# A down projection with one level of Strassen's products, its partial sums copied from bank to bank

## The chip, the core and the metric

The kernel runs on one NeuronCore of a Trainium2 chip. The metric is the device time of one execution in microseconds (us); the time of before is the median of three runs. TensorE does the matmuls into PSUM, which has eight banks here, each a tile of 128 partitions x 512 floats. VectorE and ScalarE read and write PSUM and SBUF; loads and stores are DMAs issued from the queues of SyncE (SP) and ScalarE (ACT).

## The reference

One layer of a hybrid decoder runs on 1024 prompt rows and 32 sample rows (8 sequences of 4), so on 1056 rows of 1024 channels. What is ahead of the channel mixing (two mixers, an output projection, norms) is not touched. The channel mixing is

```python
h = rms_norm(x, g_pre_ffn)
f = einsum('bsf,fd->bsd', square(relu(einsum('bsd,df->bsf', h, w_up))), w_down)
return x + rms_norm(f, g_post_ffn)
```

with w_up 1024 x 4096 and w_down 4096 x 1024. Everything is float32 in and out.

## The kernel before

**Precision.** A float32 product is made of three matmuls: each operand is split into a rounded part and the rest ("hi" and "lo", types marked fp32r), and hi·hi, hi·lo and lo·hi are summed in PSUM (`TERMS`). `split` does this: a cast on ScalarE (line 127), a subtraction on VectorE (line 128).

**Columns.** In the channel mixing rows are the moving columns. They stand in two column groups: group 0 has tiles 0 to 3 and the sample rows, 2 x 272 columns, group 1 has tiles 4 to 7, 2 x 256 columns (`SUB`). The halves of a group are the two column halves of a Strassen product.

**Up stage.** It already runs one level of Strassen (Winograd's form, seven products in place of eight). `NPAIR` = 16 pairs of row blocks, each for both groups, are 32 `Quad`s. A product is 12 matmuls (4 blocks of the inner dimension x 3 terms). Between products that accumulate on bank A, ScalarE keeps copies of A in SBUF (`snap`, line 797), and VectorE adds them later (lines 817 to 840). `first`, `second` and `third` are cut so that a Quad's first two products stand ahead of the last two of the one before. The results are squared after Relu (line 844) and stored to `f_d` in HBM, two stores for a Quad from ScalarE's queue (`store`, `flush`). `up_weights` makes the seven weight forms of a pair: four VectorE sums and seven splits.

**Down stage.** It is a plain product: `NFB` = 8 rounds of 4 row blocks of f; for each of 8 output blocks and 3 column chunks (`TB`: 400, 400 and 256 columns) `down_one` sums 12 matmuls in one of four rotating "z" banks, and VectorE adds the bank to the accumulator `acc` in SBUF (line 1077; a copy in the first round, line 1075). The next round's f blocks and weights are loaded on SyncE's queue and split meanwhile (`f_tile`, `pair`). In the last round the chunks are the outer loop, so that tiles whose columns are complete can be finished between matmuls: `Finish` transposes the accumulator on TensorE, squares on ScalarE (line 1105), multiplies with the gain on VectorE (line 1106), scales and adds x (line 1119) and stores. Seven of the nine tiles are finished inside; tiles 6 and 7 have their first half inside and their second half after the last matmul.

**Order.** Matmuls, transposes and DMAs keep the order in which the program issues them on their queue (`keep_in_program_order`). The order of VectorE's and ScalarE's instructions is fixed when the kernel is built; each engine runs its own in that order and waits at an instruction whose operands are not ready. A tile pool with `bufs=n` gives a buffer out again when its last reader is done.

Of the kernel before, what the change touches and what calls it, by code (L numbers as in the profile page):

```python
# [39 lines left out]
TB = [(0, 3 * P + NSH), (3 * P + NSH, 3 * P + NSH), (6 * P + NS, 2 * P)]  # L40
TBT = [(0, 1, 2), (NCH, 3, 4, 5), (6, 7)]
# [4 lines left out]
def hymba_step(ctx: ExitStack, tc: tile.TileContext, a: dict):  # L46
# [24 lines left out]
    hpool1 = ctx.enter_context(tc.tile_pool(name="hpool1", bufs=1, side="right"))  # L71
# [3 lines left out]
    stage = ctx.enter_context(tc.tile_pool(name="stage", bufs=3))  # L75
    psum = ctx.enter_context(tc.tile_pool(name="psum", bufs=4, space=PSUM))
# [18 lines left out]
    f_d = [dpool.tile([P, T], F32, name="f_d%d" % ft) for ft in range(NFT)]  # L95
# [673 lines left out]

    class Quad:  # L770
# [72 lines left out]
        def emit(self, i, f):  # L843
            vec.scalar_tensor_tensor(f, f, 0.0, f, ALU.max, ALU.mult)  # L844
            c0 = GBASE[self.g]
            store(f_d[2 * self.p + i][:, c0:c0 + 2 * self.n].rearrange("p (s c) -> p s c", s=2), f)
# [176 lines left out]
    def f_tile(ft):  # L1023
        f = f_pools[0 if ft % 9 < 7 else 1].tile([P, 2, T], F32R, name="f")
        for g in range(2):
            c = slice(GBASE[g], GBASE[g] + GW[g])
            raw = raw_load(f_d[ft][:, c], [P, GW[g]])
            split(f[:, 0, c], f[:, 1, c], raw)
        return f
# [4 lines left out]
    q0.sums()  # L1034
    ws_up = {0: wup0, 1: up_weights(wraw1)}
    prev = q0
    for i, (p, g) in enumerate(seq):
# [3 lines left out]
        flush()  # L1041
        if prev.g == 1:
# [7 lines left out]
        if i == len(seq) - 2:  # L1050
            psg0.close()
            phg0.close()
            f_pools.append(pq.enter_context(tc.tile_pool(name="fp", bufs=7, side="right", reuse_waits="tile")))
            fs0 = [f_tile(ft) for ft in range(FB)]
            ws0 = pair(a["w_down"][0, 0])
# [3 lines left out]
    flush()  # L1059
    pph.close()  # L1060
    pcm.close()

    with ExitStack() as pf:
        pf.enter_context(pq)
        f_pools.append(pf.enter_context(tc.tile_pool(name="fp2", bufs=2, reuse_waits="tile")))
        accp = pf.enter_context(tc.tile_pool(name="accp", bufs=1, reuse_waits="tile"))
        rp = pf.enter_context(tc.tile_pool(name="rp", bufs=2, reuse_waits="tile"))
        acc = accp.tile([P, KT, T], F32, name="acc")

        def down_one(b, fs, w, d, c0, n):  # L1070
            ps = zbank()
            run(gemm3([ps[:, :n]], [hl(w, k) for k in range(FB)], [[hl(f, slice(c0, c0 + n))] for f in fs]))
            o = acc[:, d, c0:c0 + n]
            if b == 0:
                vec.tensor_copy(o, ps[:, :n])
            else:
                vec.tensor_tensor(o, ps[:, :n], o, ALU.add)  # L1077

        class Finish:
            def __init__(self, t):  # L1080
                self.t, self.r = t, rows(t)
                self.tp = []
# [3 lines left out]
                self.ssq2 = small.tile([P, 2], F32, name="ssqo")  # L1086
                if t == NCH:
                    self.av = rp.tile([P, KT, NS], F32, name="av", bufs=1)
                    vec.tensor_copy(self.av.rearrange("p k (s c) -> p k s c", s=2),
                                    acc[:, :, 0:GW[0]].rearrange("p k (s c) -> p k s c", s=2)[:, :, :, 2 * P:])  # L1090

            def cols(self, d):
                if self.t == NCH:
                    return self.av[:, d]
                g, c = gcol(self.t)
                return acc[:, d, GBASE[g] + c.start:GBASE[g] + c.stop]

            def half(self, h):
                r = self.r
                hs = slice(h * 512, (h + 1) * 512)  # L1100
                tp = tbank()
                for k in range(4):
                    transpose(tp[:r, k * P:(k + 1) * P], self.cols(4 * h + k), P)
                junk = rp.tile([P, 512], BF16, name="rl")
                act.activation(junk[:r], tp[:r], AF.Square, scale=D ** -0.5, accum_out=self.ssq2[:r, h:h + 1])
                vec.tensor_tensor(self.y[:r, hs], tp[:r], g_fin[:r, hs], ALU.mult)  # L1106
# [16 lines left out]
        def round_weights(b, dps):  # L1123
            return [w for dp in dps for w in pair(a["w_down"][b, dp])]

        fs, ws = fs0, ws0 + round_weights(0, range(1, KT // 2))
        for b in range(NFB):
            last = b + 1 == NFB
            if not last:
                nxt = ([f_tile((b + 1) * FB + i) for i in range(FB)], round_weights(b + 1, range(KT // 2)))  # L1130
                for d in range(KT):
                    for c0, n in TB:
                        down_one(b, fs, ws[d], d, c0, n)
                fs, ws = nxt
            else:
                g_fin = unit().bitcast(F32).rearrange("p a b -> p (a b)")
# [128 lines left out]
```

## Time and profile before

| | |
|---|---|
| median of 3 runs | 1096.48 us (1095.11 to 1099.24) |
| the profiled execution's own time | 1095.61 us |
| its span, first to last instruction | 1093.9 us |
| mean granted TensorE clock | 0.997 of full speed |
| TensorE / VectorE / ScalarE busy | 1065.0 / 680.1 / 428.2 us |

A share of busy time is a mean over stages. TensorE's matmuls are pipelined, so the duration of one (323 ns, say) is longer than the distance from one to the next; rates are read from how often a fixed piece of work recurs. Idle time of an engine that isn't the bound costs nothing.

### The profile page before, as it was taken

The page shows a single profiled execution, that of the slowest core. Times are in us where ns is not written, and L with a number is a line of the kernel's source. Part 1 is how long each engine was busy: PE and PEld are TensorE (multiplying, and loading weights), DVE is VectorE, ACT ScalarE, POOL GpSimd, SP SyncE. Part 2 cuts the span into 40 slices and gives each one's busy share as a digit, 9 for nine tenths or more (in the row PEclk, how much of TensorE's full clock was granted, in tenths as well). Part 3 has the DMA queues.
Part 4 walks back from the last instruction along what each step waited for, and adds up shares of the span by engine and source line. Part 5 has one row for each costly group of instructions (what it writes and reads, how often), then busy time and mean ns, then how long its engine had stood idle before and what let it go on. Part 6 is the DMA issues. An engine that isn't in the chain of part 4 may idle for free.

```text
span 1093.9 us, 17859 instructions
## 1 busy us (share of the span) xinstructions
PE 1065.0 (97%) x7053; PEld 996.2 (91%) x7053; DVE 680.1 (62%) x1338; ACT 428.2 (39%) x936; POOL 50.7 (5%) x77
## 2 busy tenths in 40 slices
PE   7999999999999999999999999999999999999996
PEld 5788877887787899999999999999999999999996
DVE  5777886886667897566565563575463544635257
ACT  6588874656344553323323322433030211302012
POOL 1100002120100100000000000000000000000001
PEclk9999999999999999999999999999999999999998
DMA  8432301134533334333333332554150432406034
GB/s 273 149 108 78 97 25 51 47 107 148 182 120 122 111 111 126 117 96 102 118 90 107 118 94 76 186 168 145 50 157 17 142 89 68 147 10 222 1 95 165
DMA packets 52227, 121.35 MB, mean 111 GB/s; under 512 B 6944, under 2 KB 16640, under 8 KB 52128
## 3 DMA queue, kind: packets, MB, share of 16 engines
q1 hardware_dynamic: 33312, 89.44, 27.1%
q10 hardware_dynamic: 18832, 30.78, 7.5%
q8 instruction: 55, 0.90, 0.3%
q14 instruction: 28, 0.23, 0.1%
HBM read 89.43 MB, written 31.82 MB: 111 GB/s over the span
## 4 chain that ended last, share of the span: by engine, by line
PE 85%; DVE 7%; ACT 4%; issue 2%; DMA 1%; POOL 1%; SPq 0%; DVEq 0%; ACTq 0%; POOLq 0%
PE z L64 72%; PE t L64 10%; PE t L67 3%; ACT sc L527 1%; ACT w L130 1%; DVE hn L973 1%; DVE w L128 1%; DVE w L1106 1%; DVE xr L967 1%; DVE pT L128 0%; DVE w L1119 0%; POOL ro L143 0%; DMA raw<-in_w_down_dram 0%; DVE w L131 0%; DMA raw<-in_w_qkv_dram 0%
## 5 line engine op out<-in xcount | busy, mean ns | idle before, releaser
L64 PE MATMUL z<-f,w 128*128 128x400 f32 (+1 forms) x2304 | 372.1, 323 | 0.0
L64 PEld LDWEIGHTS z<-f,w 128*128 128x128 f32 x2304 | 369.6, 188 | 0.7 <-DVE acc L1077 0.4
L64 PE MATMUL z<-w,hT_hi 128*128 128x512 f32 (+1 forms) x768 | 210.2, 380 | 0.4 <-DVE raw L191 0.4
L1077 DVE TENSOR_TENSOR acc<-z,acc 128x400 f32<-128x400 f32 (+1 forms) x168 | 87.0, 522 | 139.9 <-PE z L64 139.8
L64 PEld LDWEIGHTS z<-w,hT_hi 128*128 128x128 f32 x768 | 133.7, 188 | 25.2 <-DVE raw L191 0.8
L64 PE MATMUL z<-hT_hi,w 128*128 128x272 f32 (+1 forms) x768 | 146.8, 286 | 1.4 <-ACT s L797 1.4
L64 PE MATMUL z<-w,hT_lo 128*128 128x512 f32 (+1 forms) x384 | 124.5, 378 | 0.0
L64 PEld LDWEIGHTS z<-hT_hi,w 128*128 128x128 f32 x768 | 122.0, 189 | 1.7 <-ACT s L797 1.6
L127 ACT CAST f<-raw 128x544 fp32r<-128x544 f32 x64 | 38.6, 633 | 190.3 <-PE z L64 143.8
L64 PE MATMUL z<-hT_lo,w 128*128 128x272 f32 (+1 forms) x384 | 109.4, 285 | 0.0
L64 PE MATMUL z<-sg,w 128*128 128x272 f32 (+1 forms) x768 | 105.1, 286 | 0.6 <-ACT s L797 0.6
L64 PEld LDWEIGHTS z<-sg,w 128*128 128x128 f32 x768 | 98.7, 190 | 1.3 <-ACT s L797 1.1
L797 ACT COPY s<-z 128x256 f32<-128x256 f32 (+1 forms) x93 | 35.3, 379 | 129.0 <-PE z L64 126.1
L64 PEld LDWEIGHTS z<-w,hT_lo 128*128 128x128 f32 x384 | 67.6, 188 | 14.0
L64 PEld LDWEIGHTS z<-hT_lo,w 128*128 128x128 f32 x384 | 72.8, 190 | 0.0
L128 DVE TENSOR_TENSOR w<-w 128x512 fp32r<-128x512 f32 x64 | 43.7, 691 | 30.7 <-ACT w L127 29.5
L128 DVE TENSOR_TENSOR f<-raw,f 128x544 fp32r<-128x544 f32 x64 | 43.9, 705 | 20.0 <-ACT f L127 19.9
L128 DVE TENSOR_TENSOR w<-raw,w 128x512 fp32r<-128x512 f32 x68 | 44.0, 686 | 18.8 <-ACT w L127 18.7
L127 ACT CAST w<-raw 128x512 fp32r<-128x512 f32 x68 | 38.8, 618 | 39.6 <-DMA raw<-in_w_down_dram 34.6
L64 PE MATMUL t<-sg,w 128*128 128x272 f32 (+1 forms) x384 | 52.8, 287 | 0.6 <-DVE fo L818 0.6
L64 PE MATMUL t<-hT_hi,w 128*128 128x272 f32 (+1 forms) x256 | 52.2, 285 | 0.0
L844 DVE SCALAR_TENSOR_TENSOR fo<-fo 128x544 f32<-128x544 f32 (+1 forms) x64 | 45.3, 708 | 10.8 <-ACT fo L837 8.4
(214 smaller groups left out, 1274.8 us busy)
## 6 DMA issues: line engine op xcount, KB each, us to landing
raw<-in_w_down_dram SPq DMA_DIRECT2D x32, 512.0 KB, 4.2
rw<-in_w_up_dram SPq DMA_DIRECT2D x28, 512.0 KB, 3.9
f_d<-fo ACTq DMA_DIRECT2D x32, 272.0 KB, 3.1
raw<-f_d SPq DMA_DIRECT2D x32, 272.0 KB, 2.8
f_d<-fo ACTq DMA_DIRECT2D x32, 256.0 KB, 2.9
raw<-f_d SPq DMA_DIRECT2D x32, 256.0 KB, 2.7
xT<-in_xT_prompt_dram SPq DMA_DIRECT2D x8, 512.0 KB, 5.6
raw<-in_x_prompt_dram SPq DMA_DIRECT2D x8, 512.0 KB, 4.7
```

The lines of the kernel that those rows point to most:

```text
L64: tc.keep_in_program_order(pe.matmul(out, lhsT, rhs, start=start, stop=stop, skip_group_check=resumed))
L67: tc.keep_in_program_order(pe.transpose(out, in_, ident[:n, :n]))
L127: pin(act.copy(hi, src))
L128: pin(vec.tensor_tensor(lo, src, hi.bitcast(F32), ALU.subtract))
L130: act.activation(hi, src, AF.Copy, scale=scale)
L527: act.activation(scs[kv][:, j, 0:nk], scs[kv][:, j, 0:nk], AF.Exp, scale=-1.0, bias=nm[:, h:h + 1], accum_out=lsum[:, h:h + 1])
L797: act.copy(s, self.A)
L844: vec.scalar_tensor_tensor(f, f, 0.0, f, ALU.max, ALU.mult)
L967: vec.tensor_tensor(xr[:r], hn[:r], xr[:r], ALU.add)
L973: vec.scalar_tensor_tensor(hn[:r], xr[:r], r2[:r], g_ffn[:r], ALU.mult, ALU.mult)
L1077: vec.tensor_tensor(o, ps[:, :n], o, ALU.add)
L1106: vec.tensor_tensor(self.y[:r, hs], tp[:r], g_fin[:r, hs], ALU.mult)
```

## The change

The down projection becomes one level of Strassen too. A round (`NR` = 8) takes two pairs of row blocks, which are the two inner blocks. For each of two output halves `c` and the two column groups, `step` runs the seven products, each of 12 matmuls: two output blocks `j` x two inner blocks `k` x three terms. A step uses all eight banks as four pairs A, D, C, B. Product 1 goes to A and is copied by ScalarE to C (`fork`); product 6 is added on A and A is copied to B; products 2, 7, 3 and 4 are added on C, A, B and A, product 5 has D to itself. Matmuls thus accumulate on what ScalarE has written. `gather` adds D, C, E (A after product 7), B and A to five accumulators in SBUF on VectorE; in round 0 ScalarE copies them instead. `combine` adds D to B and E at the end. `renew` is a matmul of 512 columns that writes a whole bank: four at the start, two in the last step, after transposes have used the banks. The pairs of banks change roles from step to step.

The seven forms of f are made in the up stage: `third` gets four more VectorE sums and `stores` writes seven pieces for a Quad, from SyncE's queue. `f_load` reads back seven forms for each pair and group in three pieces and splits them; three sets of f tiles rotate. `down_weights` makes seven weight forms for each round and half with the up stage's `up_weights`; the weight array is laid out for it on the host. Five tiles are finished inside the last two steps, tiles 4 to 7 after the last matmul.

```diff
-f_d = [dpool.tile([P, T], F32, name="f_d%d" % ft) for ft in range(NFT)]
+f_d = [[dpool.tile([P, 7, n], F32, ...) for g, n in enumerate(SUB)] for p in range(NPAIR)]
...
         def third(self):
             self.product(4, self.A, False, True)
             act.activation(self.fa[:, 1], self.A, AF.Relu)
-            self.emit(0, self.fa)
+            square(self.fa)
             self.product(3, self.B, False, True)
             vec.tensor_tensor(self.fb[:, 0], self.B, self.s2, ALU.add)
-            self.emit(1, self.fb)
+            square(self.fb)
+            n = self.n
+            s = stage.tile([P, D], F32, name="raw")[:, 0:3 * n].rearrange("p (i c) -> p i c", i=3)
+            f11, f21, f12, f22 = self.fa[:, 0], self.fa[:, 1], self.fb[:, 0], self.fb[:, 1]
+            vec.tensor_tensor(s[:, 0], f21, f22, ALU.add)
+            vec.tensor_tensor(s[:, 1], s[:, 0], f11, ALU.subtract)
+            vec.tensor_tensor(s[:, 2], f11, f21, ALU.subtract)
+            vec.tensor_tensor(f21, f12, s[:, 1], ALU.subtract)
+            self.forms = [(1, f11), (5, s[:, 0]), (6, s[:, 1]), (2, f12), (7, s[:, 2]), (3, f21), (4, f22)]
+
+        def stores(self):
+            d = f_d[self.p][self.g]
+            for i, f in self.forms:
+                load(d[:, POS[i]], f)
...
+    def f_load(fs, pool_=None):
+        tiles, r, g = fs
+        n = SUB[g]
+        for a0, a1 in ((0, 2), (2, 4), (4, 7)):
+            for f, p in zip(tiles, (2 * r, 2 * r + 1)):
+                raw = (pool_ or stage).tile([P, D], F32, name="raw")[:, 0:(a1 - a0) * n]...
+                load(raw, f_d[p][g][:, a0:a1])
+                split(f[:, a0:a1, 0], f[:, a0:a1, 1], raw)
+        return tiles
+
+    def down_weights(r, c, tiles):
+        for i, t in enumerate(tiles):
+            load(t, a["w_down"][2 * r + c, i])
+        return up_weights(tiles)
...
         if i == len(seq) - 2:
...
-            fs0 = [f_tile(ft) for ft in range(FB)]
-            ws0 = pair(a["w_down"][0, 0])
+            fs0 = f_load(f_tiles(0, 0, 0))
+        if i == len(seq) - 1:
+            wdn0 = down_weights(0, 0, stage_raws())
...
+        def step(r, c, g, fs, ws, inserts=(), renewed=()):
+            n = SUB[g]
+            A, D_, C, B = [[b[:, 0:n] for b in banks[2 * i:2 * i + 2]] for i in range(4)]
+
+            def product(i, bs, start):
+                w = ws[i].rearrange("p s (k c) -> p s k c", k=4)
+                for j in range(2):
+                    for k in range(2):
+                        for m, (x, y) in enumerate(TERMS):
+                            mm(bs[j], w[:, x, 2 * k + j], fs[k][:, POS[i], y], ...)
+
+            def gather(key, bs):
+                for j in range(2):
+                    o = gacc(key, g)[:, 2 * c + j]
+                    if r == 0:
+                        act.copy(o, bs[j])
+                    else:
+                        vec.tensor_tensor(o, bs[j], o, ALU.add)
+
+            def fork(dst):
+                for j in range(2):
+                    act.copy(dst[j], A[j])
...
+            product(1, A, True)
+            fork(C)
+            product(5, D_, True)
+            gather("D", D_)
+            insert(0, 6)
+            product(6, A, False)
+            if 1 in renewed:
+                renew(banks[6:8], ws[1])
+            fork(B)
+            product(2, C, False)
+            gather("C", C)
+            insert(1, 2)
+            product(7, A, False)
+            gather("E", A)
+            product(3, B, False)
+            gather("B", B)
+            insert(2, 4)
+            product(4, A, False)
+            gather("A", A)
+            banks[:] = banks[2:4] + banks[0:2] + banks[6:8] + banks[4:6]
...
+        renew(banks[4:8], wdn0[1])
+        f_cur = [fs0, f_load(f_tiles(0, 0, 1), frp)]
+        for r in range(NR):
...
+            if r + 1 < NR:
+                w_cur.append(down_weights(r, 1, stage_raws()))
+                prefetch(0)
+                step(r, 0, 0, f_cur[0], w_cur[0])
+                step(r, 0, 1, f_cur[1], w_cur[0])
+                w_nxt.append(down_weights(r + 1, 0, stage_raws()))
+                step(r, 1, 0, f_cur[0], w_cur[1])
+                prefetch(1)
+                step(r, 1, 1, f_cur[1], w_cur[1])
             else:
...
+                step(r, 1, 0, f_cur[0], w_cur[1])
+                combine(0)
+                step(r, 0, 1, f_cur[1], w_cur[0], [(1, finish(0)), (2, finish(1))])
+                step(r, 1, 1, f_cur[1], w_cur[1],
+                     [(0, finish(2)), (1, finish(3)), (2, finish(NCH))], (1,))
+        combine(1)
+        for pair_ in ((4, 5), (6, 7)):
+            fts = [Finish(t) for t in pair_]
+            for h in range(2):
                 for ft in fts:
+                    ft.half(h, banks[0])
+                    banks[:] = banks[1:] + banks[:1]
```

## Rows read from the trace of the kernel before

**Rows 1.** The page's first part: busy us, share of span, instructions.

```profile
PE 1065.0 (97%) x7053; PEld 996.2 (91%) x7053; DVE 680.1 (62%) x1338; ACT 428.2 (39%) x936; POOL 50.7 (5%) x77
```

**Rows 2.** Busy time by stretch: length, engines' busy us, granted clock, DMA share, GB/s.

```profile
478.56:499.19 20.63, 20.63 (x170) 20.63 (x169) 12.50 (x22) 6.99 (x15) 0.00 (x0) 1.00 0.35 105
752.00:1040.00 288.00, 287.97 (x1786) 287.34 (x1786) 134.10 (x243) 53.71 (x92) 0.00 (x0) 1.00 0.31 96
```

**Rows 3.** Timeline of ScalarE, up stage: start us, us, engine, line, operation.

```profile
457.93 0.39 ACT L837 ACTIVATE fo<-z 128x256 f32<-128x256 f32 x1 [0.65 <-PE z L64]
...
478.56 0.39 ACT L837 ACTIVATE fo<-z 128x256 f32<-128x256 f32 x1 [0.65 <-PE z L64]
```

**Rows 4.** Timeline of VectorE, down stage, every third add.

```profile
962.33 0.57 DVE L1077 TENSOR_TENSOR acc<-z,acc 128x400 f32<-128x400 f32 x1 [1.77 <-PE z L64]
...
968.12 0.57 DVE L1077 TENSOR_TENSOR acc<-z,acc 128x400 f32<-128x400 f32 x1 [1.76 <-PE z L64]
```

**Rows 5.** Groups by shape, down stage: count, busy us, mean ns, idle before.

```profile
L1077 DVE TENSOR_TENSOR acc<-z,acc 128x400 f32<-128x400 f32 x86 | 49.2, 573 | 81.6 <-PE z L64 81.6
L128 DVE TENSOR_TENSOR w<-raw,w 128x512 fp32r<-128x512 f32 x48 | 30.9, 686 | 13.5 <-ACT w L127 13.4
...
L1077 DVE TENSOR_TENSOR acc<-z,acc 128x256 f32<-128x256 f32 x42 | 17.7, 421 | 16.7 <-PE z L64 16.7
L128 DVE TENSOR_TENSOR f<-raw,f 128x544 fp32r<-128x544 f32 x24 | 17.3, 722 | 6.3 <-ACT f L127 6.3
```

**Rows 6.** Groups by shape, up stage.

```profile
L797 ACT COPY s<-z 128x272 f32<-128x272 f32 x29 | 11.2, 387 | 39.4 <-PE z L64 39.4
...
L825 DVE TENSOR_TENSOR fo<-z,s 128x272 f32<-128x272 f32 x9 | 3.9, 434 | 0.0
```

**Rows 7.** Timeline where the up stage ends and the down stage begins.

```profile
697.23 0.69 DVE L844 SCALAR_TENSOR_TENSOR fo<-fo 128x512 f32<-128x512 f32 x1
...
701.02 1.14 ACT L127 CAST w<-raw 128x512 fp32r<-128x512 f32 x2 [1.84 <-DMA raw<-in_w_down_dram]
...
702.48 0.39 PE L64 MATMUL z<-hT_hi,w 128*128 128x256 f32 x1 [1.43 <-ACT s L797]
...
705.45 22.79 PE L64 MATMUL z<-f,w 128*128 128x400 f32 x140
```

**Rows 8.** Timeline of VectorE, down stage, while weights are prepared.

```profile
945.02 0.57 DVE L1077 TENSOR_TENSOR acc<-z,acc 128x400 f32<-128x400 f32 x1 [0.91 <-PE z L64]
945.81 1.29 DVE L128 TENSOR_TENSOR w<-raw,w 128x512 fp32r<-128x512 f32 x2 [0.21 <-ACT w L127]
949.07 1.29 DVE L128 TENSOR_TENSOR w<-raw,w 128x512 fp32r<-128x512 f32 x2 [1.97 <-ACT w L127]
950.28 0.57 DVE L1077 TENSOR_TENSOR acc<-z,acc 128x400 f32<-128x400 f32 x1
```

**Rows 9.** Waits, 705 to 1083 us: total us, times, longest us.

```profile
DVE f L128 <- ACT f L127: 16.2, 26, 1.5
DVE w L128 <- ACT w L127: 16.1, 14, 3.1
```

**Rows 10.** The page's DMA issues: count, KB each, us from issue to landing.

```profile
raw<-in_w_down_dram SPq DMA_DIRECT2D x32, 512.0 KB, 4.2
...
raw<-f_d SPq DMA_DIRECT2D x32, 272.0 KB, 2.8
```

**Rows 11.** The end: two lines by shape (1040 to 1094 us), two of the timeline.

```profile
L1106 DVE TENSOR_TENSOR w<-t,w 128x512 f32<-128x512 f32 x16 | 10.4, 682 | 2.4 <-ACT rl L1105 2.4
...
L67 PE MATMUL t<-ident,acc 128*128 128x128 f32 x64 | 8.6, 274 | 1.6 <-DVE acc L1077 1.6
...
1079.75 3.09 PE L64 MATMUL z<-f,w 128*128 128x256 f32 x24
...
1088.20 2.74 DVE L1119 SCALAR_TENSOR_TENSOR w<-w,ro,raw 128x512 f32<-128x512 f32 x4 [0.66 <-POOL ro L143]
```

More of the change, by code (lines that the diff above doesn't have):

```diff
@@ L94, in hymba_step @@
     x2_d = dpool.tile([T, D], F32, name="x2_d")
-    f_d = [dpool.tile([P, T], F32, name="f_d%d" % ft) for ft in range(NFT)]
+    f_d = [[dpool.tile([P, 7, n], F32, name="f_d%d_%d" % (p, g)) for g, n in enumerate(SUB)] for p in range(NPAIR)]
     kv_d = dpool.tile([NS, 2 * P], F32, name="kv_d")
@@ L768, in hymba_step, with square @@
     sg = [None, None]
+    def square(f):
+        vec.scalar_tensor_tensor(f, f, 0.0, f, ALU.max, ALU.mult)
     class Quad:
@@ L1021, in hymba_step, with f_tiles, stage_raws @@
     f_pools = []
[L1023 to L1029, printed above, removed]
+    def f_tiles(s, r, g):
+        n = SUB[g]
+        return [f_pools[s].tile([P, 7, 2, SUB[0]], F32R, name="f")[:, :, :, 0:n] for _ in range(2)], r, g
+    def f_load(fs, pool_=None):
[3 more added lines that the diff above has]
+            for f, p in zip(tiles, (2 * r, 2 * r + 1)):
+                raw = (pool_ or stage).tile([P, D], F32, name="raw")[:, 0:(a1 - a0) * n].rearrange("p (i c) -> p i c", c=n)
+                load(raw, f_d[p][g][:, a0:a1])
[5 more added lines that the diff above has]
+        return up_weights(tiles)
+    def stage_raws():
+        return [stage.tile([P, D], F32, name="raw") for _ in range(2)]
+    q0.sums()
+    ws_up = {0: wup0, 1: up_weights(wraw1)}
     last = NPAIR - 2
@@ L1041, in hymba_step @@
         flush()
+        prev.stores()
         if prev.g == 1:
@@ L1058, in hymba_step @@
     q.third()
-    flush()
+    q.stores()
     pph.close()
     pcm.close()
+    phg1.close()
     with ExitStack() as pf:
@@ L1066, in hymba_step @@
         accp = pf.enter_context(tc.tile_pool(name="accp", bufs=1, reuse_waits="tile"))
+        frp = pf.enter_context(tc.tile_pool(name="frp", bufs=2, reuse_waits="tile"))
         rp = pf.enter_context(tc.tile_pool(name="rp", bufs=2, reuse_waits="tile"))
[L1068 to L1077, printed above, removed]
+        accs = {k: accp.tile([P, 4, SUB[0] + SUB[1]], F32, name="acc%s" % k) for k in "ACBED"}
@@ L1121, in end, with finish, go, combine @@
                 flush()
[L1123 to L1134, printed above, removed]
-            else:
-                g_fin = unit().bitcast(F32).rearrange("p a b -> p (a b)")
-                load(g_fin, a["g_post_ffn"].to_broadcast([P, D]))
+        def finish(t):
+            def go(bs):
+                ft = Finish(t)
+                for h in range(2):
+                    ft.half(h, bs[h])
+                ft.scale()
+                ft.end()
+            return go
+        def combine(g):
+            for k in "BE":
+                vec.tensor_tensor(gacc(k, g), gacc(k, g), gacc("D", g), ALU.add)
+        renew(banks[4:8], wdn0[1])
+        f_cur = [fs0, f_load(f_tiles(0, 0, 1), frp)]
+        w_cur = [wdn0]
+        sets = 2
+        for r in range(NR):
+            f_nxt, w_nxt = [], []
+            def prefetch(g):
+                nonlocal sets
+                if r + 1 < NR:
+                    f_nxt.append(f_load(f_tiles(0 if sets % 3 < 2 else 1, r + 1, g), frp))
+                    sets += 1
+            if r + 1 < NR:
+                w_cur.append(down_weights(r, 1, stage_raws()))
[6 more added lines that the diff above has]
+                step(r, 1, 1, f_cur[1], w_cur[1])
+            else:
+                w_cur.append(down_weights(r, 1, stage_raws()))
+                step(r, 0, 0, f_cur[0], w_cur[0])
                 for name in ("k", "v"):
@@ L1211, in _layout @@
     w_up = w_up.reshape(NPAIR, 2, 2, P, 512)
-    w_up = np.stack([np.concatenate([w_up[:, 0, 1], w_up[:, 0, 0]], axis=-1),
-                     np.concatenate([w_up[:, 1, 0], w_up[:, 1, 1]], axis=-1)], axis=1)
+    w_down = inp["w_down"][0].reshape(NR, 2, 2, P, 2, 2, 2, P).transpose(0, 5, 4, 2, 3, 1, 6, 7)
+    w_down = w_down.reshape(2 * NR, 2, 2, P, 512)
+    w_up, w_down = [np.stack([
+        np.concatenate([w[:, 0, 1], w[:, 0, 0]], axis=-1),
+        np.concatenate([w[:, 1, 0], w[:, 1, 1]], axis=-1)], axis=1) for w in (w_up, w_down)]
     return {
@@ L1242, in _layout @@
         "w_up": c(w_up),
[L1243 to L1244 removed]
+        "w_down": c(w_down),
     }
```

88 lines of the change are left out of this document (40 added, 48 removed).

## The prediction

> **What bounds the kernel now.** I read the totals of the page first, then the busy time by stretch, then the groups of the down stage kept apart by shape, then the timeline where the two stages meet and at the end. The reader should see first that TensorE is the bound: busy 97% of the span, VectorE 62% [rows 1]. In the stretches inside the up and the down stage TensorE is busy for the whole stretch at full granted clock [rows 2], so there is no wait to remove there: only fewer or shorter matmuls help, and any new wait costs its full length. VectorE is busy 134.1 of 288.0 us in the down stage, under half.
>
> **The gain.** The up stage already runs the scheme that the down stage gets: seven products of 12 matmuls, 272 columns for column group 0 and 256 for group 1. Two such sets (168 matmuls) take 478.56 − 457.93 = 20.63 us, by the start of the same Relu one set pair apart [rows 3], with TensorE never idle [rows 2]. After the change the down stage is 8 rounds x 2 output halves x 2 column groups = 32 steps of 84 matmuls of just these widths: 16 x 20.63 = 330.1 us. Today it is 64 row-block and output-block pairs of 36 matmuls, each 968.12 − 962.33 = 5.79 us [rows 4], 370.4 us. To this come transposes inside the stage. 64 take 8.6 us [rows 11], 0.134 each; 40 remain inside (five tiles finished inside instead of seven, all halves): 5.4 us. Six renewing matmuls of 512 columns are not in the trace; a 400-column one takes about 0.18 us (5.79 us is 24 of these and 12 of 256 columns at 3.09 / 24 = 0.13 or less [rows 11]), so they are about 0.23 each, 1.4 together. New: 336.9 us. Old, from the first down matmul at 705.45 [rows 7] to the end of the last at 1079.75 + 3.09 = 1082.84 [rows 11]: 377.4 us. TensorE's own work shrinks by **40.5 us**. The columns fall by one eighth but the number of matmuls rises from 2304 to 2688, which is why 12.5% of columns become 10.9% of time.
>
> **What the other engines get.** VectorE per round (four steps, 41.26 us of TensorE):
> - 40 adds from PSUM to the accumulators, 20 of 272 columns (434 ns [rows 6]) and 20 of 256 (421 ns [rows 5]): 17.1 us. Today a round has 24, 16 of 400 columns at 573 ns and 8 of 256: 12.5 us.
> - two weight sets, each 7 subtractions and 4 sums of 512 columns at 686 ns [rows 5]: 15.1 us. Today 8 subtractions, 5.5 us.
> - activation splits: seven forms in place of four blocks. Per column group four subtractions of two forms (about 544 columns, 722 ns [rows 5]) and two of three forms; 272 more columns add about 0.28 us (573 − 421 = 152 ns for 144 columns), so 1.0 us: 4.9 us, twice: 9.7 us.
>
> Together 41.9 us, 102% of TensorE's 41.26. Back to back an instruction starts before the last one's row has ended: from the two subtractions at 949.07 to the add at 950.28 it is 1.21 us [rows 8], 0.605 each against rows of 0.686. With 0.08 us less for each of 74 instructions the round is 36.0 us. So VectorE goes from under half to between **87% and 102%** of TensorE's time in the six steady rounds.
>
> [...]
>
> **Where VectorE reaches TensorE.** Every bank is in use. The adds of the product before last and of the last must be done before the next product on the same bank. Since banks come in pairs filled one after the other, an add has half a product and one product of room: 0.74 + 1.47 = 2.2 us (one product is 20.63 / 14). Today four rotating banks give over 5 us. The trace shows what matters: at 947.10 VectorE had nothing running and waited 1.97 us for a weight cast; the add due one 2.2 us block after the one at 945.02 began only at 950.28, 3 us late [rows 8]. TensorE did not notice; with 2.2 us of room it would. Over the old stage VectorE waits 16.2 + 16.1 us behind ScalarE's casts [rows 9], 3.5 us in each 41 us, and most such casts were themselves waiting for a load. I also expect the load to be uneven: the first step of a round has the second weight set (nine of its eleven instructions, about 6 us), the rest of the last activation split (2 us), the start of the next (1.3 us) and its own adds; those due by the end of the sixth product add 3.3 us. That is 12.6 us by single rows, 10.8 back to back, wanted in some 9.9 us.
> Price per steady round: at best nothing (36.0 us fit, and prefetched forms can wait for a lighter step); at worst 41.9 + 3.5 − 41.3 = 4.1 us, and 1.6 us more if the overflow of the first step isn't won back, 5.7. I take 2.0, below the middle since the old stage's delayed adds still came between the prefetch's pairs and back to back [rows 8]: 6 x 2.0 = **12 us** (0 to 34).
>
> **ScalarE.** Per step four copies of a bank into another; no row copies PSUM to PSUM. The nearest, PSUM to SBUF, takes 387 ns for 272 columns [rows 6]; I take that, with nothing and twice that as ends. A pair, 0.78 us, must fit the same 2.2 us. ScalarE's round is 16 x 0.39 + 14 x 0.62 + 12 casts at about 0.7 = 23 us of 41: hidden, except when a cast waiting for a load sits ahead of the copy, as at 702.48, where TensorE waited 1.43 us for a copy behind casts that waited 1.84 us for w_down [rows 7]. That is in the ends above. [...]
>
> **Up stage.** Each set adds four VectorE sums of 272 columns, at most 0.43 us each: 12.5 + 3.4 = 15.9 us of 20.63 [rows 2]. No product waits for them within 10 us; seven stores per set move from ScalarE's queue to SyncE's, ahead of the next weights' load, which has a set's time to spare. 0 (0 to 3).
>
> **Handover and round 0.** The weights of the first step now need both raw tiles and eleven VectorE instructions before form 5 exists; their loads stand on SyncE behind the stores of the last set but one. That set's square ends at 697.92 [rows 7]; four sums, 1.7 us, to 699.6; the load 4.2 us [rows 10] to 703.9; cast and subtraction to 705.2, in time for product 1; form 5 comes four VectorE instructions, one cast and one subtraction later, at 709.3 against 706.9: 2.4 us late at best. The six activation loads ahead of them share three buffers, two turns of 2.8 [rows 10] + 1.4 us, which makes this later; take 5. Round 0's second activation set is loaded through buffers that lie where the up stage's tiles lay, in three turns of about 4.2 us: take 2 more. **7 us** (2 to 14).
>
> **Last round and tail.** The last round also has heavy first steps and one renewal that waits for VectorE's last reader: **3 us** (0 to 6). Today 11.1 us pass from the last down matmul to the end of the span, with two tiles to finish. Then four remain: two adds 0.85, two sums of 1024 columns 2.5, eight products with the gain at 0.68 [rows 11] 5.5, eight halves of the last step at 0.69 (four in 2.74 [rows 11]) 5.5, small ones 0.6: 15.0 us on VectorE, 3 us for the last store as now (1093.9 − 1090.94), 1.6 for work left over: 19.6, **+8.5** (+5 to +12).
>
> **Sum**, against the profiled execution's own 1095.61 us (0.9 under the median shown): 1095.6 − 40.5 + 12 + 7 + 3 + 8.5 = 1085.6, so **1086 us**. All lower ends give 1062, all upper ones 1124.
>
> **Rivals.**
> 1. *It flows like the up stage*: no steady loss, short handover, about 1070 us (1085.6 − 12 − 4). For: the up stage's TensorE never idles. Against: VectorE has 61% there, 87% or more here. 16%.
> 2. *Gain given back*: VectorE's delays cost about 3.7 us in each steady round, 1095 us: no change. For: 3.5 us of waiting behind casts per round today. 25%.
> 3. *VectorE becomes the bound: slower.* Place: the adds that free the accumulating banks in each round's first step. Price 5.7 us a round: 1085.6 + 6 x 3.7 = 1108. It decides from 4.7 us a round on (1102 us). For: 102% by single rows. Against: back-to-back starts and the lighter steps. 25%.
> 4. *The products run slower than in the up stage* (narrow matmuls bound by weight loads, say): excluded nearly by [rows 3], 1%.
>
> **How the numbers follow.** My forecast, 1077 to 1091, gets 33%; with rival 1 faster by over 0.5% (about what a measurement of this kernel can tell from no change, some 5.5 us) has 49%, no change 25%, slower 26% with rival 4. The range leaves out the far ends: 1067 to 1109.
>
> **What would show it.** Right: 32 steps near 10.3 us of matmul work, VectorE above 85% there, TensorE's few idle spells released by VectorE's adds and falling in each round's first step; an idle spell of some us where f first meets w; a tail near 20 us. Wrong: TensorE idle behind ScalarE's bank copies or behind loads in every step, bank copies well over 0.39 us, the granted clock falling between steps, or waits in the up stage for the stores.

## The result, and the profile after

The kernel after takes **1167.22 us** (median of 4 runs, 1166.81 to 1167.91) against 1096.18 us for the kernel before beside it: ratio 1.0644, 95% interval 1.0622 to 1.0666. Forecast were 1086 us and a range of 1067 to 1109: wrong in sign, and outside the range. The profiled execution took 1167.12 us, its span is 1165.4 us, its mean granted clock 0.967 (0.997 before).

I cut the span at three points: the first down matmul (705.45 us before [rows 7], 752.06 after), the end of the last one (1082.84 and 1145.07) and the end of the span (1093.9 and 1165.4).

| stage | before | after | difference | forecast |
|---|---|---|---|---|
| all up to the first down matmul | 705.45 | 752.06 | +46.6 | +5 |
| down stage | 377.4 | 393.0 | +15.6 | -23.5 |
| tail | 11.1 | 20.3 | +9.2 | +8.5 |

(The forecast column sorts the prediction's terms: 5 of the handover's 7 us stand ahead of the first down matmul; -40.5 + 12 + 2 + 3 = -23.5 in the down stage.) Two stages are wrong by some 40 us each.

The page's totals of after, to be held against [rows 1]:

```profile
PE 1060.0 (91%) x7443; PEld 982.7 (84%) x7443; DVE 833.1 (71%) x1707; ACT 531.7 (46%) x1184; POOL 50.8 (4%) x77
```

and its busy time by stretch, one in the up stage, one of four down rounds, to be held against [rows 2]:

```profile
380.00:745.00 365.00, 334.25 (x2610) 331.09 (x2608) 239.60 (x466) 109.48 (x243) 0.86 (x1) 0.96 0.39 127
...
866.00:1058.00 192.00, 173.77 (x1352) 171.60 (x1352) 150.83 (x299) 85.28 (x169) 0.00 (x0) 0.96 0.38 125
```

TensorE, which was idle for 1.2 of the 320 us from 380 to 700 us before and for none inside the down stage [rows 2], now stands for 31 of 365 and 18 of 192 us, and the granted clock is 0.96: part of its busy time is at a lower clock too. The waits of after say for whom it stands (total us, times, longest us; the first two lines are from the up stage, the others from the down stage):

```profile
PE z L64 <- ACT s L801: 18.3, 8, 3.7
PE z L64 <- ACT w L128: 11.3, 2, 5.8
...
PE z L64 <- DVE accE L1126: 21.6, 6, 4.0
PE z L64 <- DVE accA L1126: 7.9, 5, 6.6
PE z L64 <- ACT t L1130: 2.5, 4, 1.1
```

**Up stage.** TensorE waits for ScalarE's copies of bank A, 18.3 us where before it waited 0.6 us for one such copy (380 to 700 us). The 11.3 us of the second line are two waits for the weights themselves (5.80 us up to 419.14 and 5.54 us up to 710.83), each behind a cast that waited over 4 us for its load. The timeline around one of the waits for a copy in after:

```profile
634.36 0.87 SPq L51 DMA_DIRECT2D rw<-in_w_up_dram  x2
...
638.56 1.14 ACT L128 CAST w<-rw 128x512 fp32r<-128x512 f32 x2 [3.85 <-DMA rw<-in_w_up_dram]
...
642.35 2.18 ACT L128 CAST w<-w 128x512 fp32r<-128x512 f32 x4 [2.35 <-DVE w L901]
...
644.95 0.36 ACT L801 COPY s<-z 128x256 f32<-128x256 f32 x1
645.36 2.93 PE L64 MATMUL z<-sg,w 128*128 128x256 f32 x12 [3.71 <-ACT s L801]
```

The load of a pair's weights is issued at 634.36 and ScalarE waits 3.85 us for it. Behind that stand the sums of the weight forms on VectorE and four casts that wait for them; the 0.36 us copy comes last in ScalarE's fixed order, and TensorE has stood 3.71 us by then. Then 12 matmuls take 2.93 us, at a granted clock of 0.50; 12 of the same width take 1.60 at 1.00 (from 638.62). Why the load is issued so late is on SyncE's queue (a line is a run of DMAs; the last ones of a run of 14 stores):

```profile
491.33 0.80 SPq L51 DMA_DIRECT2D f_d<-raw  x2
492.18 0.44 SPq L51 DMA_DIRECT2D f_d<-fo  x1
...
497.63 0.88 SPq L51 DMA_DIRECT2D f_d<-fo  x2
498.60 0.88 SPq L51 DMA_DIRECT2D rw<-in_w_up_dram  x2
```

Around these rows a store occupies the queue for 0.33 to 0.45 us once its data are there, and it waits there for VectorE's squares and sums until they are. From 380 to 715 us the queue waits 84.6 us in 26 times for the first of the four new sums alone, which itself needs the set's last squares. In before the same queue held only loads (380 to 720 us), issued ahead; its ten waits from 437 to 521 us are all for VectorE's last reads of their buffers:

```profile
437.39 82.86 SPq L51 DMA_DIRECT2D rw<-in_w_up_dram  x9
```

**Down stage.** One long wait a round, in rounds 2 to 6 at the last product of the round's first step, which adds on the banks that accE is read from. (Round 1's comes in the step after: 6.60 us up to 821.67, for accA, behind preparation that fills VectorE from 811.96 to 820.49.) The timeline of one in after:

```profile
902.74 1.14 ACT L128 CAST w<-raw 128x512 fp32r<-128x512 f32 x2 [2.17 <-DMA raw<-in_w_down_dram]
903.39 1.29 DVE L129 TENSOR_TENSOR w<-raw,w 128x512 fp32r<-128x512 f32 x2 [2.01 <-ACT w L128]
...
907.64 2.49 DVE L129 TENSOR_TENSOR w<-w 128x512 fp32r<-128x512 f32 x4
...
910.65 1.35 DVE L129 TENSOR_TENSOR f<-raw,f 128x544 fp32r<-128x544 f32 x2
911.92 0.78 DVE L1126 TENSOR_TENSOR accD<-z,accD 128x272 f32<-128x272 f32 x2
912.62 0.78 DVE L1126 TENSOR_TENSOR accC<-t,accC 128x272 f32<-128x272 f32 x2
913.32 0.78 DVE L1126 TENSOR_TENSOR accE<-z,accE 128x272 f32<-128x272 f32 x2
913.80 6.38 PE L64 MATMUL z<-f,w 128*128 128x272 f32 x38 [4.04 <-DVE accE L1126]
```

From 903.39 to 911.92 VectorE does nothing but weights and activation splits. Six adds stand behind them, and then run back to back. TensorE stands 4.04 us for the fifth. The same wait ends at 865.72, 913.80, 961.18, 1007.90 and 1056.55: a round is (1056.55 - 865.72) / 4 = 47.7 us, 6.4 over its 41.26 us of matmuls. Busy time in steps of 2 us shows the rest of that price (the third figure from the end is the granted clock):

```profile
910.00:912.00 2.00, 0.00 (x0) 0.00 (x0) 2.00 (x5) 0.60 (x1) 0.00 (x0) 1.00 0.00 0
912.00:914.00 2.00, 0.20 (x1) 0.20 (x2) 2.00 (x7) 0.00 (x0) 0.00 (x0) 0.95 0.75 205
914.00:916.00 2.00, 2.00 (x9) 2.00 (x10) 1.64 (x5) 0.76 (x2) 0.00 (x0) 0.50 0.37 148
916.00:918.00 2.00, 2.00 (x14) 2.00 (x14) 1.44 (x3) 0.92 (x2) 0.00 (x0) 0.70 0.68 184
918.00:920.00 2.00, 2.00 (x19) 2.00 (x18) 0.59 (x3) 1.36 (x3) 0.00 (x0) 1.00 1.03 401
```

After 4 us of standing still TensorE goes on at a granted clock of 0.50: 23 matmuls begin in the 4 us from 914, where 38 would at the rate after 918. That is some 1.6 us on top of a wait of 4, an estimate from these counts.

**Tail.** 20.3 us, as priced: four tiles are left, eight halves, and VectorE, busy 16.0 us of it, does them one after the other.

### The profile page after: what moved, and what is told of

It reads as the page before. It is cut to its first block, busy times and chain, and to the rows that moved or that the text cites. A ratio compares the mean times of both kernels' runs of the same rounds, so it can differ in the third digit from the quotient of the medians.

```text
span 1165.4 us, 19447 instructions
## 1 busy us (share of the span) xinstructions
PE 1060.0 (91%) x7443; PEld 982.7 (84%) x7443; DVE 833.1 (71%) x1707; ACT 531.7 (46%) x1184; POOL 50.8 (4%) x77
## 3 DMA queue, kind: packets, MB, share of 16 engines
q1 hardware_dynamic: 70176, 132.72, 34.8%
## 5 line engine op out<-in xcount | busy, mean ns | idle before, releaser
L64 PE MATMUL z<-f,w 128*128 128x272 f32 (+1 forms) x1920 | 263.5, 295 | 39.4 <-DVE accE L1126 21.6
L64 PEld LDWEIGHTS z<-f,w 128*128 128x128 f32 x1920 | 252.2, 198 | 45.0 <-DVE accE L1126 23.0
L64 PE MATMUL z<-hT_hi,w 128*128 128x272 f32 (+1 forms) x768 | 153.5, 294 | 11.9 <-ACT w L128 11.3
L128 ACT CAST f<-raw 128x544 fp32r<-128x544 f32 (+3 forms) x96 | 67.3, 707 | 96.5 <-DMA raw<-f_d 65.7
L129 DVE TENSOR_TENSOR f<-raw,f 128x544 fp32r<-128x544 f32 (+3 forms) x96 | 75.2, 795 | 42.0 <-ACT f L128 41.6
L64 PE MATMUL t<-f,w 128*128 128x272 f32 (+1 forms) x768 | 104.1, 285 | 0.0
L64 PEld LDWEIGHTS t<-f,w 128*128 128x128 f32 x768 | 97.9, 189 | 0.0
L128 ACT CAST w<-w 128x512 fp32r<-128x512 f32 x128 | 71.0, 617 | 51.2 <-DVE w L901 46.2
L129 DVE TENSOR_TENSOR w<-w 128x512 fp32r<-128x512 f32 x128 | 80.3, 683 | 0.2 <-ACT w L128 0.2
L1130 ACT COPY t<-z 128x256 f32<-128x256 f32 (+1 forms) x128 | 46.6, 366 | 68.1 <-PE z L64 64.8
```

What stands on the lines that cost most here:

```text
L64: tc.keep_in_program_order(pe.matmul(out, lhsT, rhs, start=start, stop=stop, skip_group_check=resumed))
L128: pin(act.copy(hi, src))
L129: pin(vec.tensor_tensor(lo, src, hi.bitcast(F32), ALU.subtract))
L1130: act.copy(dst[j], A[j])
```

## The experiments

The kernel before ran beside each group of runs at 1096.47 us (experiments 1, 2, 4 and 5), 1096.72 (3, 6, 7 and 8), 1096.65 (9, 10 and 11) and 1096.68 (12).

**1. The loads ahead of the stores** (`e1_loads_first`): the weights' loads of the up stage are issued before the seven stores.

```diff
+        raws = up_raws(prev.p + 2) if prev.g == 1 and prev.p + 2 < NPAIR else None
         prev.stores()
         if prev.g == 1:
             del ws_up[prev.p]
-            if prev.p + 2 < NPAIR:
-                ws_up[prev.p + 2] = up_weights(up_raws(prev.p + 2))
+            if raws:
+                ws_up[prev.p + 2] = up_weights(raws)
```

> The changed kernel with one edit in the up stage: the two loads of the next weights are put on SyncE's queue ahead of the seven stores of the set that has just ended, not behind them. Queue theory: the up stage's loss of some 45 us comes from these loads, which stand behind fourteen stores that wait for VectorE; ScalarE's casts then wait for them with the bank copies behind. It expects 1125 to 1145 us and TensorE's waits for the bank copies (18 us in the changed kernel) mostly gone. VectorE theory (the four added sums and their buffers hold the up stage up): 1160 us or more, waits as they were.

1132.49 us, ratio 1.0329 (1.0313 to 1.0344): 34.7 us less than after, by one move on a queue. The first down matmul comes at 716.18 and not 752.06; the down stage stays as it was (393.8 us to 1109.93). TensorE's waits up to 715 us in this run:

```profile
PE z L64 <- ACT s L801: 3.4, 4, 1.0
PE t L64 <- ACT w L128: 1.9, 1, 1.9
```

The 18.3 us behind copies are 3.4, and the two long waits for weights are gone. ScalarE itself still waits 41.5 us for these loads (43.4 in after): what went is not its waiting, but that the copies stand behind it. Since the engines' orders are fixed when the kernel is built, moving the loads also moved the casts among the copies; the run doesn't separate these two.

**2. The four sums alone** (`e2_before_sums`): the kernel before with the four VectorE sums for each set, results unused.

```diff
         def third(self):
...
+            vec.tensor_tensor(s[:, 0], f21, f22, ALU.add)
+            vec.tensor_tensor(s[:, 1], s[:, 0], f11, ALU.subtract)
+            vec.tensor_tensor(s[:, 2], f11, f21, ALU.subtract)
+            vec.tensor_tensor(s[:, 0], f12, s[:, 1], ALU.subtract)
```

> The kernel before with the four added VectorE sums of each set alone, into a staging buffer that nobody reads; stores, loads and the whole down stage as before. It computes nothing new. Queue theory: no change, 1094 to 1099 us, since VectorE stays under 80% in the up stage. VectorE theory: 1115 us or more, with TensorE waiting in the up stage.

1097.57 us, ratio 1.0014 (1.0004 to 1.0023). By themselves the sums cost some 1 us: hidden, nearly as forecast.

**3. The queue alone** (`e8_before_sync_stores`): the kernel before with its two stores for each set on SyncE's queue.

```diff
-            store(f_d[2 * self.p + i][:, c0:c0 + 2 * self.n].rearrange(...), f)
+            load(f_d[2 * self.p + i][:, c0:c0 + 2 * self.n].rearrange(...), f)
```

> The kernel before with one edit: the two stores of each set are issued from SyncE's queue, in line with the loads, not from ScalarE's. Nothing else of the change is in it. Queue theory: the next weights' loads now stand behind stores that wait for VectorE, and the up stage loses some time, 1102 to 1130 us (fewer stores than in the change, and ready earlier). If the queue matters only together with the four sums: 1094 to 1100 us.

1107.89 us, ratio 1.0096 (1.0067 to 1.0125), all of it ahead of the down stage: the first down matmul is at 718.11, the down stage takes 377.4 us as in before. Its queue:

```profile
480.32 8.02 SPq L51 DMA_DIRECT2D f_d<-fo  x4
488.43 0.91 SPq L51 DMA_DIRECT2D rw<-in_w_up_dram  x2
```

The loads stand 8 us behind four stores (14 stores in after). Two stores a set on the wrong queue cost 11 us without any of the new work. ScalarE's order is fixed anew when this kernel is built, so this run doesn't separate the late loads from that order either.

**4. The preparation one step later** (`e3_prefetch_later`): each group of loads and splits is written after the step that it stood ahead of.

```diff
-                w_cur.append(down_weights(r, 1, stage_raws()))
-                prefetch(0)
                 step(r, 0, 0, f_cur[0], w_cur[0])
+                w_cur.append(down_weights(r, 1, stage_raws()))
                 step(r, 0, 1, f_cur[1], w_cur[0])
-                w_nxt.append(down_weights(r + 1, 0, stage_raws()))
+                prefetch(0)
                 step(r, 1, 0, f_cur[0], w_cur[1])
...
```

> The changed kernel with the preparation of weights and activation forms written one step later in each round of the down stage, so that the accumulator adds of the step in front come first on VectorE; the same instructions in all. Order theory (the adds wait behind a burst of preparation in each round's first step, 4 us, and the granted clock falls afterwards): 1115 to 1140 us, no wait of TensorE for the add of E above 2 us. Load theory (VectorE has simply too much work in a round): 1155 to 1170 us, the wait turns up in another step.

1159.82 us, ratio 1.0581 (1.0564 to 1.0598), only 7.4 us less. The long waits for accE are gone, but TensorE now waits 13.9 us in 12 waits for ScalarE's copies from bank to bank and 9.9 us in 11 for accA. The burst was moved, not spread. By its time and by the wait that turns up elsewhere this is the load theory's side (1155 to 1170), and so is the next run (1120 or more); experiment 6 decides between them.

**5. Both** (`e4_both`): experiments 1 and 4 together.

> Both edits of the two other kernels of the changed down stage: loads ahead of the stores in the up stage, preparation one step later in the down stage. If queue and order theory hold and their gains add: 1070 to 1100 us, at or under the kernel before. If VectorE's amount of work is what counts: 1120 us or more.

1121.02 us, ratio 1.0228 (1.0211 to 1.0245): the two add (34.7 + 7.4 = 42.1, measured 46.2). The waits of this run, at most 1.82 us from 760 to 1050 us, leave the clock there at 1.00. Two lines of this run, a step of 2 us by busy time and the wait that falls into it:

```profile
944.00:946.00 2.00, 0.27 (x3) 0.06 (x1) 2.00 (x4) 2.00 (x5) 0.00 (x0) 1.00 0.00 0
946.00:948.00 2.00, 1.91 (x16) 1.91 (x17) 2.00 (x6) 0.04 (x1) 0.00 (x0) 1.00 0.03 8
```

TensorE stood 1.82 us until 946.09 and went on at 1.00.

**6. The adds first** (`e5_adds_first`): experiment 1, and the copies from bank to bank and the adds into the accumulators get priority over the preparation in the order of their engines.

```diff
-                    if r == 0:
-                        act.copy(o, bs[j])
-                    else:
-                        vec.tensor_tensor(o, bs[j], o, ALU.add)
+                    with tc.high_priority():
+                        if r == 0:
+                            act.copy(o, bs[j])
+                        else:
+                            vec.tensor_tensor(o, bs[j], o, ALU.add)
...
-                    act.copy(dst[j], A[j])
+                    with tc.high_priority():
+                        act.copy(dst[j], A[j])
```

> The changed kernel with the loads ahead of the stores in the up stage, and in the down stage ScalarE's bank copies and the accumulator adds given a higher priority in the fixed order than the preparation of weights and forms; preparation written where the change has it. Base of comparison: the kernel with the loads ahead alone, 1132.5 us. Order theory (the adds and copies stand behind preparation that they need not wait for): 1085 to 1105 us, no wait of TensorE for the add of E above 1.5 us, granted clock at full speed in the six middle rounds. Load theory (VectorE has too much work): 1120 us or more.

1103.55 us, ratio 1.0055 (1.0037 to 1.0073), 28.9 us less than experiment 1; the down stage falls from 393.8 to 365.3 us (716.02 to 1081.36). VectorE's timeline in the heavy part of a round, in this run:

```profile
910.80 0.68 DVE L904 TENSOR_TENSOR w<-raw 128x512 f32<-128x512 f32 x1
...
911.41 0.42 DVE L1128 TENSOR_TENSOR accC<-t,accC 128x256 f32<-128x256 f32 x1
911.74 0.68 DVE L901 TENSOR_TENSOR w<-raw,w 128x512 f32<-128x512 f32 x1
...
912.34 0.42 DVE L1128 TENSOR_TENSOR accC<-t,accC 128x256 f32<-128x256 f32 x1
912.67 0.41 DVE L1128 TENSOR_TENSOR accE<-z,accE 128x256 f32<-128x256 f32 x1
913.11 0.69 DVE L129 TENSOR_TENSOR w<-w 128x512 fp32r<-128x512 f32 x1
```

The adds now come between single pieces of the preparation. Its busy time by stretch:

```profile
725.00:1025.00 300.00, 294.37 (x2350) 289.14 (x2350) 243.27 (x478) 161.44 (x334) 0.00 (x0) 1.00 0.43 138
```

The same weight load recurs every 42.97 us (from 837.18 to 1009.05 in four rounds): 1.7 us lost a round. VectorE is busy 81%, so 34.8 us a round. This is the order theory's side: the same work, in another order. Both engines' orders were changed at once; the waits that went were above all for VectorE (accE and accA, 29.3 us in experiment 1 and 1.0 here), while those for bank copies were 2.1 us and are 2.6.

**7. The adds first and the preparation later** (`e6_adds_first_later`): experiment 5 with the priority of 6.

> The same priority, with the preparation also written one step later; base 1121 us. Order theory: it takes away the waits for bank copies (15 us) and for the add of A (7 us) that were left: 1090 to 1105 us. If these waits come from loads that land late, not from the order: 1115 us or more.

1104.35 us, ratio 1.0067 (1.0052 to 1.0082): no better than 6. Once the adds go first, it doesn't matter in which step the preparation stands.

**8. No weight preparation** (`e7_one_weight_set`): experiment 1, with round 0's two weight sets used in every round; later rounds' weights are neither loaded nor cast nor summed, so the run takes work from the queue, from ScalarE and from VectorE.

```diff
-                w_cur.append(down_weights(r, 1, stage_raws()))
+                if r == 0:
+                    w_cur.append(down_weights(r, 1, stage_raws()))
...
-                w_nxt.append(down_weights(r + 1, 0, stage_raws()))
+                w_nxt = w_cur
```

> The kernel with the loads ahead in the up stage, base 1132.5 us; in the down stage the two weight sets of round 0 are used in every round: it leaves out the loads, casts, sums and subtractions of 14 of the 16 sets, some 15 us of VectorE's work a round, and computes with the wrong weights from round 1 on. If VectorE's burst of preparation is what delays the adds, the six waits for the add of E go, with the fall of the clock that follows: 1085 to 1100 us. If the rounds lose time in another way (narrow matmuls, bank copies, f loads), 1115 us or more.

1086.74 us, ratio 0.9908 (0.9886 to 0.993): 45.8 us less than experiment 1, without any priority. The down stage takes 347.8 us (718.79 to 1066.63), 10.9 over the 336.9 of its matmuls. Busy time of this run by stretch:

```profile
725.00:1025.00 300.00, 294.68 (x2388) 292.33 (x2388) 173.06 (x346) 114.05 (x250) 0.00 (x0) 1.00 0.35 106
```

**9. The priority alone** (`e11_adds_first_alone`): the diff of 6 on the kernel after, the loads left behind the stores.

> The kernel after, with only the forwarding copies and the adds into the accumulators put ahead of the other work of their engines; the loads stay behind the seven stores. Theory (two separate faults, one in the up stage and one in the down stage, which add): the down stage loses the 29 us that it lost in the run with the loads first, and the up stage nothing, 1138 us (1134 to 1143), with the down stage starting at 750 to 754. Rival (the loads' queue is behind both, and the adds gain only where weights come in time): less than 15 us gained, above 1152.

1143.9 us, ratio 1.0434 (1.0415 to 1.0454). The first down matmul stays late (751.39) and the down stage falls to 368.8 us (to 1120.21): two faults in two stages, which add, but for some 6 us: 23.3 us gained here, 28.9 with the loads first. The time is 0.9 us above the range that was given for it.

**10. Weights loaded earlier** (`e9_weights_earlier`): experiment 6, with the first round's down weights loaded ahead of the seven stores issued with them, the last round's ahead of the f loads of the round before.

```diff
+        raws0 = down_raws(0, 0) if i == len(seq) - 1 else None
         prev.stores()
...
+                raws1 = down_raws(r + 1, 1) if r + 2 == NR else None
                 prefetch(1)
```

> This is the version with the loads ahead of the stores and the adds ahead of the preparation (1103.55 us), and two sets of down weights are loaded earlier: the first round's ahead of the seven stores at the handover, the last round's ahead of the six f loads of the round before. What is left in that version beside the tail is two waits of TensorE for weights (3.17 and 1.62 us at the handover, 4.25 and 1.51 in the last round), each followed by a stretch at the lower clock level. Theory (these waits come from the place of the loads in the queue): both go with most of the lower clock behind them, 5 to 12 us less, 1092 to 1098. Rival (the f loads, now later, are late in their place, or the writing of the weights and not their load is what is late): no more than 3 us less, 1100 to 1106.

1103.6 us, ratio 1.0063 (1.0048 to 1.0078): nothing gained, the rival's side. The last round's long wait went (4.25 us before, 0.34 at the same place now), but the first round's load is still issued only at 709.88 (709.42 in experiment 6): it now stands behind five f loads, the last of them issued by 705.8, and shares their buffers. The waits for these weights at the handover stay (0.41, 3.58 and 0.73 us, for 3.17 and 1.62), and eight waits of 0.34 to 0.99 us for f come between 734 and 747 us, where experiment 6 has one.

**11. The sums at the end first** (`e10_combine_first`): experiment 10 with priority for `combine`.

```diff
-                vec.tensor_tensor(gacc(k, g), gacc(k, g), gacc("D", g), ALU.add)
+                with tc.high_priority():
+                    vec.tensor_tensor(gacc(k, g), gacc(k, g), gacc("D", g), ALU.add)
```

> As the run with the weights loaded earlier, and the four adds that merge the fifth accumulator into two others (two for each group of tokens) are also put ahead of the other work of VectorE. In the version of 1103.55 the tail took 20.3 us, and TensorE waited 3.22 us in it for the second of these adds, which ran 3 us after its input was there, behind the last tile's norm. Theory (the order on VectorE sets this wait): 2 to 4 us less than the run with the weights earlier. Rival (what VectorE does first it then does not do for the norm, and the tail is set by VectorE's whole work): within 1 us of it.

1106.72 us, ratio 1.0082 (1.0051 to 1.0114); its runs spread from 1101.63 to 1108.75. That is neither's number. The wait of 3.22 us for the last sum is gone, and from the last down matmul's end (1083.19 + 1.66) to the end of the span it is still 20 us, with VectorE busy 15.7 us of it in both runs: this wait did not set the tail, VectorE's work did. The 3 us that the run is longer lie in the down stage (369.6 us, 366.3 in experiment 10) and were not followed further.

**12. Buffers of their own** (`e12_own_buffers`): as 10, but the first round's weights are loaded one set sooner, into two buffers of the up stage that are free by then.

```diff
+        if i == len(seq) - 2:
+            raws0 = down_raws(0, 0, [rawp.tile([P, D], F32, name="rw") for _ in range(2)])
         prev.stores()
```

> As the version with the loads ahead of the stores and the adds ahead of the preparation (1103.55 us). The last round's weights are loaded ahead of the f loads, as in the run with the weights earlier, where this wait of 4.25 and 1.51 us went; but the first round's weights get two buffers of the up stage that are free by then, and are loaded one set sooner, so that they neither wait behind the stores nor keep the f loads from their buffers, which cost that run some ten small waits of TensorE for f between 734 and 747 us. Theory (what is left at the handover is the late load; the earlier run gave its gain back by the f loads it held up): 6 to 14 us less, 1089 to 1097, level with before or just ahead of it. Rival (the first round's weights are late because their forms need weight units that the last pairs still hold, or because VectorE is full there, whenever they are loaded): 1097 to 1102.

1096.34 us (12 runs, 1091.6 to 1098.47), ratio 0.9992 (0.9981 to 1.0003): 7.2 us less than 6, inside the theory's range, and level with before. TensorE goes from the up stage into the down stage without a gap:

```profile
714.67 1.60 PE L64 MATMUL t<-sg,w 128*128 128x256 f32 x12
716.11 1.22 PE L64 MATMUL t<-w 128*128 128x512 f32 x4
717.16 4.67 PE L64 MATMUL z<-f,w 128*128 128x272 f32 x36
```

By the three cuts against before: +11.7 us up to the first down matmul (717.16), 357.6 us in the down stage (to 1074.79), which is 19.8 less, and a tail of 20.3, 9.2 more. Sum +1.1 us, but for rounding the difference of the spans (1095.1 and 1093.9).

## Why the prediction was wrong

**The gain: right.** With the weights' preparation out of the way the down stage came to within 10.9 us of the 336.9 reckoned (experiment 8). No product ran slower by itself (rival 4): in the 300 us shown for experiment 8 a matmul took 294.68 / 2388 = 0.123 us, as in the up stage of before (20.63 / 168). Of the excess, 5.3 us are waits in these 300 us, at a granted clock of 1.00; the rest lies ahead of and behind them.

**Up stage, "seven stores per set move from ScalarE's queue to SyncE's, ahead of the next weights' load, which has a set's time to spare. 0 (0 to 3)": this step failed.** It was worth 35 us (experiment 1). I gave the load a set's time to spare and put no price on the queue: a load behind stores is issued when VectorE has done the last of their data, and then only after 14 issues of some 0.44 us. ScalarE's casts follow the load, and the copies of bank A follow the casts; that a cast waiting for a load holds up a copy was named from [rows 7], but applied to the down stage's copies alone. Experiment 3 shows the price of the move without any new work (11 us for two stores a set), experiment 2 that the sums without the move cost some 1 us. How much of the 35 us is the late load itself and how much the casts' place ahead of the copies stays open; the two waits for weights, 11.3 us, are the late load's.

**Steady rounds, "I take 2.0, below the middle": mis-sized.** Measured 6.4 us a round, outside the bound of 5.7 too. The place is rival 3's: the adds that free the accumulating banks in each round's first step. Its reason, VectorE as the bound, is not what the runs show. Two things were missing. The bounds had no price for the clock after a wait (about 1.6 us of the 6.4). And the delay was reckoned as overflow of a step with too much work, while the fixed order put nearly all of one preparation ahead of the adds: 8.5 us in one piece, where 2.2 us of room were reckoned, with the total fitting. That it fits was underrated: VectorE's round took 34.8 us, below the lower end of the 36.0 to 41.9, and with the adds first a round loses 1.7 us. So the 2.0 describes experiment 6, in which VectorE has the same work in another order.

**Round 0 and the last round: 2 and 3 us forecast.** What exceeds the forecast in the down stage, 15.6 + 23.5 = 39.1 us, is 6 x 4.4 = 26 us of steady rounds and some 13 us here, where TensorE waits 6.1 us in round 0 and 5.0 us in the last round (spells of 0.3 us or more; the rest was not separated). **Handover:** weights late by waiting behind the stores, as reckoned; with loads first, 10.7 us pass in all ahead of the first down matmul (716.18 - 705.45), of which the handover's own share was not separated. Experiment 12 closes the gap at that point, yet 11.7 us remain ahead of it: in the stretch from 380 to 700 us its TensorE is busy 5.4 us less than in before (313.37 and 318.80), with 7.5 us of waits for copies up to 715 us. Of the 11.7 us, 7.0 are waits up to 715 us beyond those of before (9.6 and 2.6 us) and 1.05 the four renewing matmuls; some 3.7 stay open.

**Tail: right,** 9.2 for 8.5, and by the working given: VectorE is busy 16.0 us in it, for 15.0 + 1.6 reckoned, and experiment 11 shows that the one long wait there is not what sets it.

**ScalarE's copies: right.** A copy from bank to bank took 373 ns for 272 columns, for the 387 taken; in the same trace the copies from a bank to SBUF took 382 to 391 (five groups of four). So the copy into a bank took 9 to 18 ns less than one into SBUF here.

**Sum.** 1167.1 - 1085.6 = 81.5 us of error: 41.6 ahead of the down stage, 39.1 in it, 0.7 in the tail. Either fault alone would have left the time outside the range: 1132 us with the up stage mended, 1144 with the down stage's order mended. With both mended it is 1104, inside.

## What to carry to other kernels

When a store is moved to a queue that issues loads, price the loads: here each stood behind the stores' data (84.6 us of the queue's waits for one sum alone), not behind their bytes (0.33 to 0.45 us of queue for a store, 1.8 until it lands), and the copies that ScalarE had behind the load in its fixed order were late with it (TensorE waited 18.3 us for them; 3.4 with the loads first). When banks or buffers give an engine 2 us of room, ask in which order its work is laid out before asking whether it fits: here the same work cost 6.4 us a round in bursts and 1.7 with the freeing instructions first. And a saving of one eighth of the matmuls' columns is worth what the stages around it leave: of 40.5 us here 20 survived in the best version, and the longer tail and the slower start took those.

## What the hardware showed beside this

Long waits of TensorE cost more than their length here: after one of 4.04 us the granted clock was 0.50 to 0.70 for 4 us, after one of 1.82 us it stayed at 1.00. Length alone does not decide it: in after, one of 2.44 us (up to 553.25) left the clock at 1.00 until 561, one of 2.30 us (up to 691.67) was followed by 0.50 from 693 to 695. Between 760 and 1050 us experiment 5 waited 23.3 us, at most 1.8 us at a time, at a granted clock of 1.00, and experiment 1 30.8 us, up to 6.7 us at a time, at 0.94; their down stages took 383.0 us (715.66 to 1098.66) and 393.8, so 7.5 of the difference of 10.8 are the waits themselves. SyncE's issue of a store took 0.33 to 0.45 us, which makes fourteen of them some 5 to 6 us of queue.
